# New rules for a build-time planner that orders the in-projection and the delta rule

## The chip, the cores and the metric

The kernel runs on one core of a Trainium2 chip. The metric is device time in microseconds for one execution, taken as the median of several runs. The profile is one such execution, recorded by the hardware profiler.

The engines are named as in the profile: PE is TensorE (matmul), DVE is VectorE, ACT is ScalarE, POOL is GpSimd, SP is SyncE, which here only issues DMAs. Each engine works through its own list of instructions in order; between engines there are semaphores.

## The reference

One residual block on a sequence of 1024 tokens of width 1024, batch 1, all in float32:

```python
mod = c_act @ w_ada + b_ada                       # shift1, scale1, gate1, shift2, scale2, gate2
h = rms_norm(x, norm1_w) * (1 + scale1) + shift1
p = h @ w_in                                      # q, k, v, z (4 heads x 128), a, beta, sc_b, sc_c, sc_h
qkv = silu(causal_depthwise_conv(p[:, q|k|v], width 4))
g = -exp(A_log) * softplus(a + dt_bias);  beta = sigmoid(b)
o = gated_delta_rule_chunked(l2(q), l2(k), v, g, beta)    # chunks of 64
o = rms_norm(o, gdn_norm_w) * silu(z)
y_sc = sc_b * causal_depthwise_conv(sc_c * sc_h, width 3)
x = x + gate1 * (concat[o, y_sc] @ w_out)
h = rms_norm(x, norm2_w) * (1 + scale2) + shift2
x = x + gate2 * ((silu(h @ w_gate) * (h @ w_up)) @ w_down)     # inner width 2816
return rms_norm(x, norm_f_w)
```

Inside the delta rule each chunk needs the inverse of a unit lower triangular 64 x 64 matrix (`triangular_solve` in the reference):

```python
lmat = where(strict, (k * beta) @ k.T * decay, 0)
tmat = triangular_solve(lmat, eye, lower=True, unit_diagonal=True)
u = tmat @ (v * beta);  w = tmat @ (k * beta * exp(g))
# scan over chunks:
v_new = u - w @ S;  out = q_dec @ S + attn @ v_new;  S = S * exp(g_last) + k_dec.T @ v_new
```

## The kernel before

The sequence is worked in two halves of 512 tokens, called hf 0 and 1. Activations stand transposed, 128 channels on the partitions and 512 tokens along a row. A float32 product is made of three fp32r matmuls of 512 columns, on a high and a low part of each operand: `h` holds the normalised input's parts, `u` (or `L`, `wu`) a weight's. A weight block is loaded as `raw`, cast to its high part on ACT or DVE, and the low part is a DVE subtraction.

The program has three parts. A short start and the feed-forward part (lines L87 and L88) are issued in an order that is written by hand. Between them, for roughly the first 475 us, the in-projection, the delta rule, the out-projection and the conditioning vectors are written as some forty small tasks (`ab_phase`, `stage_a`, `gdn`, `merge`, `output`, `load_y`, `coordinator` and so on). Each is ordinary code that asks the class `Sim` before every instruction. `Sim` keeps a clock for each engine while the kernel is built, prices every instruction (`cost`), works out when its operands are ready (`ready`) and when it could start (`start_of`), and issues next the instruction that can start first, by the tasks' priorities among near ties (`run`). `MARGIN` is a time that it adds to what a PE instruction waits for. So the numbers in `Sim` do nothing on the chip; they only set the order in which each engine gets its instructions. All instructions of this part have one line in the profile, that of the common helper: L452 before, L464 after.

The steps which the prediction follows:

- `ab_phase(hf)` multiplies `h` with the few columns for a and b (tile `ab`), copies the result out of PSUM as `raw`, turns it (`abt`), and computes the decay `G` from it on DVE, ACT and PE.
- `stage_a` makes each head's chunk matrices `kk`, `qk`, its decays from `WQ` (loaded from `g_scr`), `L` and `at`, with exponentials on ACT.
- `gdn(hf)` waits for all heads, loads the 16 x 16 x 64 diagonal blocks into `A` and inverts them by forward substitution on DVE (pairs of rows `qs<-A` and `A<-A,qs`, 30 steps). The result is turned, for hf 0 by DMAs through DRAM (`dx` into `xbd`), for hf 1 in `turned` by two DVE transposes and by copies on ACT and POOL. From `xbd` come `DD` (tile `qs`, transposed once more) and `XA` (tile `A`). `merge` then joins the blocks on PE in two levels (`P`, `Q`, `PP`, `Tt`); the first instruction of it on PE is `P<-qs,L`.
- The scan over chunks has on PE `A`, `O`, `V` and `K`. `output` squares `O` on ACT (`jk`, `so`), takes the root on POOL (`ro`), scales `u`, and turns it (`y`).
- `w_out_units` and `load_y` fetch the weights and the rows of y for the out-projection `o<-h,L`; `y_scr` is a scratch in DRAM, the four jobs of `y1` fetch the second half of its first four blocks into `WQ`. `coordinator` opens memory pools and loads `x2`, the input again, for the residual sum.

Of the kernel before, what the change touches and what calls it, by code (L numbers as in the profile page):

```python
# [35 lines left out]
PIPE0 = 8.25  # L36
AHEAD_T = 0.5
HOLD = dict(pe=0.0, dve=0.12, act=0.12, sp=0.0, pool=0.0)
MARGIN = dict(pe=0.6)
BIAS = dict(dve=0.3)  # L40
PR = dict(sums0=0.35, x0=0.1, ada0=0.2, h0=0.3, late=0.31, w0=0.4, acc=0.5, load0=0.0, setup=0.2, hurry=0.5, chain=0, m=1, evac=1.2, a=2, v=2.5, ab=1.2, out=4, h1=1.3, split=3, y0=5, wu=5.5, x2=6, ada=7, fill=9)
TASKS = "z00 q30 q20 s00 z12 z32 z22 z01 q31 q11 q01 q21 s32 s22 s10 s11 s01".split()
# [9 lines left out]
def kernel(  # L52
# [253 lines left out]
    class Sim:  # L306
        ENG = {"pe": "pe", "dve": "dve", "act": "act", "pool": "pool", "sp": "sp"}

        def __init__(self, chain_, start):
            self.chain, self.t, self.table = chain_, dict(start), "Silu"  # L310
            self.acc, self.owner, self.hist = {}, {}, {}
            self.tasks, self.pipe, self.now, self.cur = [], 0.0, 0.0, None
            self.back = threading.Semaphore(0)
            self.lock = []
            self.log, self.idle = [], {}

        def res(self, tag, n, ids=None):
            return Res(self, tag, range(n) if ids is None else ids)

        def own(self, t, res, i, t0=0.0):  # L320
            self.owner[t.tensor.name] = (res, i)
            if t0:
                self.acc[t.tensor.name] = [[0, P, 0, 1 << 30, t0, True, None]]
# [32 lines left out]
        def region(self, ap):  # L356
# [15 lines left out]
                    hi += s * (n - 1)  # L372
            return name, p0, p0 + dims[0][1], lo, hi + 1, ap.space == bass.MemoryType.DRAM

        def cost(self, eng, op, a, k):
            outs, ins = [], []
            pos = [v for v in a if hasattr(v, "tensor")]
            if "out" in k:
                outs.append(k["out"])
            else:  # L380
                outs.append(pos.pop(0))
            ins += pos
            for n, v in k.items():
                if n != "out" and hasattr(v, "tensor"):
                    (outs if n == "accum_out" else ins).append(v)
            o = outs[0]
            n = o.free_size()
            table = None
            if eng == "pe":
                if op == "transpose":  # L390
                    busy = 0.107
                else:
                    fast = ins[1].dtype == F32R
                    busy = max(n * 0.000443, 0.107) if fast else max(n * 0.00168, 0.224)
                lat = busy + 0.30
            elif op == "dma_start":
                busy, lat = 0.44, None
            elif eng == "act":
                big = max([n] + [v.free_size() for v in ins])
                busy = 0.15 + (0.1 if hasattr(k.get("scale"), "tensor") else 0.0) + big * 0.0007 + (0.19 if "accum_out" in k else 0.0)  # L400
                lat = busy + 0.25
                func = [v for v in a if isinstance(v, type(AF.Silu)) and v in (AF.Silu, AF.Exp, AF.Ln)] if op == "activation" else []
                if func:
                    table = str(func[0]).split(".")[-1]
            elif eng == "pool":
                busy = 1.1 if op == "tensor_tensor" else 0.1 + n * 0.0009 if op == "memset" else 0.65 if n >= 256 else 0.5
                lat = busy + 0.15
            else:
                big = max([n] + [v.free_size() for v in ins])
                sb = all(v.space != PSUM for v in outs + ins)  # L410
                if op == "memset":
                    busy = 0.08 + n * 0.0005
                elif sb and op in ("tensor_copy", "tensor_scalar"):
                    busy = 0.08 + n * 0.00062
                else:
                    busy = 0.08 + big * 0.00104 + (0.05 if op == "scalar_tensor_tensor" else 0.0)
                if "accum_out" in k:
                    busy += 0.1
                lat = busy + 0.15
            return outs, ins, busy, lat, table  # L420

        def ready(self, eng, outs, ins):
            t = 0.0
            for w, aps in ((True, outs), (False, ins)):
                for ap in aps:
                    name, p0, p1, f0, f1, dram = self.region(ap)
                    for a in self.acc.get(name, ()):
                        if (w or a[5]) and a[0] < p1 and p0 < a[1] and a[2] < f1 and f0 < a[3]:
                            if eng == "pe" and a[6] == "pe" or dram and w or eng == "dma" and w and a[5] and a[6] == "dma":
                                continue  # L430
                            t = max(t, a[4])
            return t
# [24 lines left out]
        def start_of(self, way):  # L457
            eng, (outs, ins, busy, lat, table), at = way
            if at is None:
                at = way[2] = self.ready("dma" if lat is None else eng, outs, ins) + MARGIN.get(eng, 0.0)  # L460
            t = max(at, self.t[eng])
            return t + 1.28 if table and table != self.table else t

# [33 lines left out]
        def run(self):  # L497
            while True:
# [25 lines left out]
                if lat is None:  # L524
                    run_ = min(n_ for n_ in (ap.ap[-1][1] * 4 for ap in outs + ins))
                    self.pipe = max(t + DMA_T[0], self.pipe) + outs[0].nbytes() / (150e3 if run_ <= 128 else 290e3 if run_ <= 1024 else 380e3)
                    end = rd = self.pipe + DMA_T[1]
                else:
                    end, rd = t + lat, t + busy + 0.1
                self.idle.setdefault(eng, []).append((self.t[eng], t, busy, task["name"], "", outs[0].tensor.name))  # L530
# [310 lines left out]
        spread_cols(RS, rs1, rs_scr)  # L841
        done.add("x1")

    h1_left = list(range(KB))

    def h1_work():
        sim.wait(lambda: "x1" in done)
        while h1_left:
            k = h1_left.pop(0)
            h = h_slot(k, 1)  # L850
            hf = hfs.tile(sp, [P, HT], F32, "hf")
            DVE.scalar_tensor_tensor(hf, x1t[k // 2][:, k % 2], s1c[:, k:k + 1], RS, ALU.mult, ALU.mult)
            ACT.activation(h[:, 0, :], hf, AF.Identity, bias=b1c[:, k:k + 1])
            DVE.scalar_tensor_tensor(h[:, 1, :], hf, b1c[:, k:k + 1], h[:, 0, :].bitcast(F32), ALU.add, ALU.subtract)
            free(hf)
            H[k][1] = h
            if all(H[j][1] is not None for j in range(KB)):
                done.add("h1")
# [135 lines left out]
    M_ORD = (4, 5, 6, 7, 0, 1, 2, 3)  # L994
    sq_acc = []

    held, n_wout = [], [0]

    def ev_o(ps, m):
        sim.wait(lambda: ("x2", m) in done and "g1" in done)  # L1000
        x_ = x2[m][:, 0:HT]
        DVE.scalar_tensor_tensor(x_, ps, g1c[:, m:m + 1], x_, ALU.mult, ALU.add)
# [200 lines left out]
    def gdn(hf):  # L1203
# [32 lines left out]
        for p in range(2):  # L1236
            for c in range(2):
                q = 64 * c + 32
                ecopy(DD[64 * c + 32 * p:64 * c + 32 * p + 32, 0], xbd[0][q:q + 32, p::2, q:q + 32])
        for p in range(2):  # L1240
            for c in range(2):
                q, m, r = 64 * c + 32 - 32 * p, Q_AT[p, c], 64 * c
                POOL.tensor_copy(XA[q:q + 32, :, m:m + 32], xbd[0][r:r + 32, p::2, r:r + 32])
        DVE.transpose(flat(DD[:, 1]), flat(DD[:, 0]))
        for h in heads:
            sim.spawn(merge, PR["m"], hf, h, T, XA, DD)
        sim.wait(lambda: all(("mq", hf, h) in done for h in heads))
# [97 lines left out]
    def w_unit(k, ch, take, out_):  # L1345
# [2 lines left out]
        n_wout[0] += 1  # L1348
        if n_wout[0] == 2 * KB:
            done.add("wout")  # L1350
            for kw, m in held:
                seq("sp", nc.sync.dma_start(**kw))
                done.add(("x2", m))
        hi, lo = take()
        if k < 4:
            escale(hi, r, gnc)
# [25 lines left out]
    def take_lx(n):  # L1382
        def take():
            sim.wait(lambda: all(("uw", 1, h) in done for h in heads))
            if len(xbd) == 1:
                xbd.append(gp.tile([P, 4, HT], F32R, name="wu", tag="xbd", bufs=1))
            return gt("L", (P, HT), F32R), xbd[1][:, n, :]
        return take

    def take_wq():  # L1390
        t = gt("WQ", (P, 2, HT), F32R)
        return t[:, 0, :], t[:, 1, :]

# [16 lines left out]
            sim.spawn(series, PR["wu"], jobs)  # L1410

    def y1():
        sim.wait(lambda: ("chain", 1) in done)
        jobs = [(load_y, k, 1, take_wq) for k in KORD[:4]]
        for _ in range(2):
            sim.spawn(series, PR["y0"], jobs)
# [3 lines left out]
    def coordinator():  # L1420
# [16 lines left out]
            gp.tile([P, 4, P], F32, name=nm("L_0"), tag=f"L{i}", bufs=1)  # L1437
        for i in range(2):
            POOL.memset(xbd[0][:, 8 * i:8 * i + 8, :], 0.0)
        done.add("gp")  # L1440
        sim.wait(lambda: "filled" in done and live[0] == 0 and all(("vt", 1, h) in done for h in heads) and
                 all(("sc", i, hf) in done and ("z", i, hf) in done for i in range(4) for hf in range(2)))
        b1.__exit__(None, None, None)
        pools["x2"] = tc.tile_pool(name="x2p", bufs=1, side="right", reuse_waits="tile")
        x2p = pools["x2"].__enter__()
        for t in range(NT):
            x2.append(x2p.tile([P, D], F32, name=f"x2_{t}", tag=f"x2_{t}"))
        for i, m in enumerate(M_ORD):
            sim.wait(lambda: len(us1) + len(us0) > min(5 + i, 12))
            if i < 2 or "wout" in done:  # L1450
                dma(x2[m], x_t[m])
                done.add(("x2", m))
            else:
                sim.op("sp", "dma_start", lambda **kw: held.append((kw, m)) or [], (), dict(out=x2[m], in_=x_t[m]))

    gp = x2p = b1p = None
    x2 = []
# [1184 lines left out]
```

## Time and profile before

| | us |
|---|---|
| median of 3 runs (lowest, highest) | 1144.19 (1143.35, 1146.99) |
| profiled execution, whole | 1145.62 |
| its span, first to last instruction | 1143.8 |
| PE busy in it | 1126.6 |
| DVE, ACT, POOL busy | 948.6, 612.1, 99.3 |
| mean granted TensorE clock | 0.998 |

A row of the timeline has its start, its length, the engine, the line, the operation, the tile that it writes, the tiles that it reads, and in brackets the idle time of that engine just before it with what ended it. A row may stand for several like instructions (x4). Tile names are those of the program without their numbers. Ends of matmuls are modelled, so two matmuls that follow each other overlap a little in the records.

### The profile page before, as it was taken

To read this page: it belongs to the slowest core of one execution; us is meant where nothing else is said; L and a number is where in the kernel's file an instruction comes from. 1 tells how busy PE (TensorE), PEld (TensorE's weight loads), DVE (VectorE), ACT (ScalarE), POOL (GpSimd) and SP (SyncE) were. 2 spreads that over 40 slices of the span, in tenths; PEclk is the share of its full clock that TensorE was granted. 3 is DMA by queue.
4 is the path that set the end of the run, shared out by engine and by line. 5 is a ranking of instruction groups with operands and counts; after the bars stand their busy time and mean duration, and the time that the engine had idled before them with its cause. 6 is when DMAs were issued, how large, how long until landed. Compare 5 with 4: busy or idle time off the path is not lost.

```text
span 1143.8 us, 17102 instructions
## 1 busy us (share of the span) xinstructions
PE 1126.6 (98%) x5660; PEld 951.2 (83%) x5660; DVE 948.6 (83%) x1909; ACT 612.1 (54%) x1372; POOL 99.3 (9%) x150
## 2 busy tenths in 40 slices
PE   9998999999999999999999999999999999999997
PEld 7887888898888897888888888888888888888885
DVE  7798879889989856699988998878888886689976
ACT  7686863649733643255544544545454476454344
POOL 0010100101100201000010010101010000000302
PEclk9999999999999999999999999999999999999999
DMA  9933256655355472440367667876677599669933
GB/s 367 353 102 102 79 171 192 177 180 183 116 180 174 159 279 68 74 148 19 139 181 210 171 187 177 233 197 162 183 207 200 138 329 362 206 177 355 289 136 147
DMA packets 164978, 214.65 MB, mean 188 GB/s; under 512 B 52589, under 2 KB 81305, under 8 KB 164889
## 3 DMA queue, kind: packets, MB, share of 16 engines
q1 hardware_dynamic: 155832, 198.69, 53.4%
q0 software_dynamic: 7712, 14.42, 8.0%
q8 instruction: 44, 0.72, 0.3%
q10 hardware_dynamic: 1344, 0.46, 0.2%
q14 instruction: 46, 0.37, 0.1%
HBM read 163.94 MB, written 60.58 MB: 196 GB/s over the span
## 4 chain that ended last, share of the span: by engine, by line
PE 90%; ACT 3%; DVE 3%; DMA 1%; issue 1%; POOL 0%; SPq 0%; ACTq 0%; DVEq 0%
PE acc L87 36%; PE acc L452 24%; PE dn L87 16%; PE o L87 4%; PE o L452 3%; DVE xo L88 1%; PE O L452 1%; PE P L452 1%; PE Q L452 1%; PE V L452 1%; PE qk L452 1%; DMA raw<-y_scr 1%; PE K L452 1%; PE A L452 1%; ACT L L452 1%
## 5 line engine op out<-in xcount | busy, mean ns | idle before, releaser
L452 PE MATMUL acc<-h,u 128*128 128x512 f32 x1200 | 293.6, 396 | 0.0
L452 PEld LDWEIGHTS acc<-h,u 128*128 128x128 f32 x1200 | 220.4, 188 | 42.4
L87 PE MATMUL acc<-h,hl 128*128 128x512 f32 (+1 forms) x540 | 109.1, 353 | 0.1
L87 PEld LDWEIGHTS acc<-h,hl 128*128 128x128 f32 x540 | 90.3, 189 | 15.1 <-issue 0.5
L87 PE MATMUL acc<-h,u 128*128 128x512 f32 (+1 forms) x516 | 100.4, 345 | 0.0
L87 PE MATMUL acc<-T,hl 128*128 128x512 f32 x408 | 97.6, 391 | 0.3 <-DVE T L88 0.3
L87 PEld LDWEIGHTS acc<-h,u 128*128 128x128 f32 x516 | 84.7, 189 | 12.6
L87 PE MATMUL acc<-T,u 128*128 128x512 f32 x384 | 91.2, 390 | 0.0
L87 PE MATMUL dn<-h,h 128*128 128x512 f32 x396 | 90.7, 389 | 0.0
L87 PEld LDWEIGHTS acc<-T,hl 128*128 128x128 f32 x408 | 75.2, 188 | 15.8 <-DVE T L88 0.8
L87 PEld LDWEIGHTS dn<-h,h 128*128 128x128 f32 x396 | 74.4, 188 | 15.4
L87 PEld LDWEIGHTS acc<-T,u 128*128 128x128 f32 x384 | 71.0, 188 | 14.1
L452 ACT CAST u<-raw 128x512 fp32r<-128x512 f32 x68 | 41.9, 619 | 53.9 <-PE acc L452 46.5
L452 DVE TENSOR_TENSOR u<-raw,u 128x512 fp32r<-128x512 f32 x82 | 56.6, 692 | 6.4 <-ACT u L452 5.8
L88 ACT COPY L<-acc 128x256 f32<-128x256 f32 x68 | 25.3, 372 | 64.4 <-PE acc L87 64.0
L88 ACT CAST h<-rw 128x512 fp32r<-128x512 f32 x60 | 35.1, 619 | 40.8 <-PE dn L87 26.3
L88 DVE TENSOR_TENSOR xo<-xo,dn 128x512 f32<-128x512 f32 x66 | 44.9, 684 | 14.1 <-PE dn L87 13.6
L452 DVE SCALAR_TENSOR_TENSOR cv<-pr,cols_a,cv 128x512 f32<-128x512 f32 x72 | 53.0, 749 | 1.5 <-ACT cv L452 1.3
L88 DVE TENSOR_TENSOR h<-rw,h 128x512 fp32r<-128x512 f32 x60 | 39.7, 687 | 15.6 <-ACT h L88 15.6
L452 DVE SCALAR_TENSOR_TENSOR raw<-raw,cb 128x512 f32<-128x512 f32 x64 | 43.8, 686 | 4.3 <-DMA raw<-in_w_mod_dram 3.9
L88 DVE TENSOR_TENSOR cc<-cc,acc 128x512 f32<-128x512 f32 x66 | 41.3, 646 | 4.9 <-PE acc L87 4.9
L88 ACT COPY cc<-acc 128x512 f32<-128x512 f32 x64 | 35.2, 585 | 19.0 <-PE acc L87 19.0
(399 smaller groups left out, 2193.0 us busy)
## 6 DMA issues: line engine op xcount, KB each, us to landing
raw<-in_w_in_dram SPq DMA_DIRECT2D x82, 256.0 KB, 3.4
am_scr<-cc SPq DMA_DIRECT2D x75, 256.0 KB, 2.2
raw<-in_w_mod_dram SPq DMA_DIRECT2D x64, 256.0 KB, 3.1
rw<-am_scr SPq DMA_DIRECT2D x53, 256.0 KB, 5.3
R<-in_w_gate_dram SPq DMA_DIRECT2D x22, 512.0 KB, 5.1
R<-in_w_up_dram SPq DMA_DIRECT2D x22, 512.0 KB, 5.9
rw<-bm SPq DMA_DIRECT2D x43, 256.0 KB, 5.3
wa<-in_w_mod_dram SPq DMA_DIRECT2D x16, 512.0 KB, 9.3
```

Source lines behind the costliest of these rows:

```text
L87: return call(*a, **k)
L88: ins = call(*a, **k)
L452: ins = call(*a, **k)
```

## The change

Nothing that is computed changes. The edits are of three kinds.

1. The planner's rules. `ready` has each engine wait for all accesses of another engine to the same PSUM tile, whichever part of the tile they touch, and lets ACT, DVE and POOL overwrite what they wrote themselves without waiting. `start_of` keeps a DMA back until the eighth last has landed. `gone` tells when memory comes free that a new pool takes over, for the first pool's slots, for `x2` and for the second use of `xbd`. `MARGIN` for PE goes from 0.6 to 1.0.
2. The planner's prices: dearer POOL roots and strided copies, strided copies on ACT, strided DVE transposes, activations with a bias, and `tensor_scalar`; cheaper short sums on ACT.
3. The tasks: `y1` starts when all weights of the out-projection are under way, and waits for the end of the second chain only before it takes `WQ`; `x2` loads are issued by the coordinator as out-projection tiles begin, instead of being held in a list; in `gdn` the transpose of `DD` is written ahead of the copies to `XA`.

```diff
-MARGIN = dict(pe=0.6)
+MARGIN = dict(pe=1.0)
...
+        def gone(self, aps):
+            return max([a[4] for ap in aps for a in self.acc.get(ap.tensor.name, ())] + [self.now])
...
+            apart = lambda ap, n: n >= 256 and ap.space != PSUM and abs(ap.ap[-1][0]) > 1 and ap.ap[-1][1] > 1
...
-                busy = 0.15 + (0.1 if hasattr(k.get("scale"), "tensor") else 0.0) + big * 0.0007 + (0.19 if "accum_out" in k else 0.0)
+                busy = 0.15 + 0.09 * sum(hasattr(k.get(n_), "tensor") for n_ in ("scale", "bias")) + big * 0.0007
+                busy += (0.06 if n <= P else 0.19) if "accum_out" in k else 0.3 if apart(ins[0], n) else 0.0
...
-                busy = 1.1 if op == "tensor_tensor" else 0.1 + n * 0.0009 if op == "memset" else 0.65 if n >= 256 else 0.5
+                busy = 1.35 if op == "tensor_tensor" else 0.1 + n * 0.0009 if op == "memset" else 1.03 if apart(ins[0], n) else 0.7 if n >= 256 else 0.42
...
-                    busy = 0.08 + big * 0.00104 + (0.05 if op == "scalar_tensor_tensor" else 0.0)
+                    busy = 0.08 + big * 0.00104 + (0.05 if op in ("scalar_tensor_tensor", "tensor_scalar") else 0.0)
+                if op == "transpose" and apart(ins[0], n):
+                    busy += n * 0.00104
...
                     for a in self.acc.get(name, ()):
+                        if ap.space == PSUM and a[6] not in (eng, None):
+                            t = max(t, a[4])
+                            continue
                         if (w or a[5]) and a[0] < p1 and p0 < a[1] and a[2] < f1 and f0 < a[3]:
-                            if eng == "pe" and a[6] == "pe" or dram and w or eng == "dma" and w and a[5] and a[6] == "dma":
+                            if eng == "pe" and a[6] == "pe" or dram and w or eng == "dma" and w and a[5] and a[6] == "dma" or \
+                                    w and a[6] == eng and eng in ("act", "dve", "pool"):
                                 continue
...
-                at = way[2] = self.ready("dma" if lat is None else eng, outs, ins) + MARGIN.get(eng, 0.0)
+                at = way[2] = max(self.ready("dma" if lat is None else eng, outs, ins) + MARGIN.get(eng, 0.0), 0.0 if lat else self.landed[-8])
...
+        DVE.transpose(flat(DD[:, 1]), flat(DD[:, 0]))
         for p in range(2):
             for c in range(2):
                 q, m, r = 64 * c + 32 - 32 * p, Q_AT[p, c], 64 * c
                 POOL.tensor_copy(XA[q:q + 32, :, m:m + 32], xbd[0][r:r + 32, p::2, r:r + 32])
-        DVE.transpose(flat(DD[:, 1]), flat(DD[:, 0]))
...
     def take_wq():
+        sim.wait(lambda: ("chain", 1) in done)
         t = gt("WQ", (P, 2, HT), F32R)
...
     def y1():
-        sim.wait(lambda: ("chain", 1) in done)
+        sim.wait(lambda: "wout" in done)
...
-            if i < 2 or "wout" in done:
-                dma(x2[m], x_t[m])
-                done.add(("x2", m))
-            else:
-                sim.op("sp", "dma_start", lambda **kw: held.append((kw, m)) or [], (), dict(out=x2[m], in_=x_t[m]))
+            if i > 1:
+                sim.wait(lambda: "wout" in done or len(begun) >= i)
+            dma(x2[m], x_t[m])
+            done.add(("x2", m))
```

What this does to the order is read from the two programs' instruction lists. On ACT, at the second `ab_phase` (`raw<-ab` copies its result out of PSUM; `WQ`, `L`, `at` are decays of the first half's heads), the list before is

```order
L452 COPY ch_1190<-acc_1130 128x512
L452 ACTIVATE h_1_275_1178<-hf_1179,b1c 128x512
L452 ACTIVATE h_1_271_1156<-hf_1157,b1c 128x512
L452 CAST u_1217<-raw_1194 128x512
L452 ACT_TABLE_LOAD
L452 ACTIVATE WQ_1254<-WQ_1254 128x512
L452 ACTIVATE L_1246<-L_1246,G_1090 128x128
L452 COPY raw_1284<-ab_1236 128x512
```

and after

```order
L464 COPY ch_1189<-acc_1130 128x512
L464 CAST u_1214<-raw_1192 128x512
L464 ACTIVATE h_1_275_1179<-hf_1180,b1c 128x512
L464 COPY raw_1284<-ab_1242 128x512
L464 CAST u_1293<-raw_1218 128x512
L464 ACTIVATE cv_1315<-ch_1189,cols_a 128x512
L464 ACT_TABLE_LOAD
L464 ACTIVATE WQ_1260<-WQ_1260 128x512
```

The copy out of PSUM has moved from behind the table load and two exponentials to a place ahead of them.

On PE, at the start of `merge` for the second half, before:

```order
L452 MATMUL acc_4216<-h_1_210_842,u_4123 128x512 x3
L452 MATMUL acc_4216<-h_1_211_843,u_4123 128x512 x3
L452 MATMUL acc_4216<-h_1_227_930,u_4123 128x512 x3
L452 MATMUL acc_4216<-h_1_235_979,u_4123 128x512 x3
L452 MATMUL acc_4216<-h_1_246_1038,u_4151 128x512 x3
L452 MATMUL acc_4216<-h_1_263_1118,u_4151 128x512 x3
L452 MATMUL acc_4216<-h_1_271_1156,u_4151 128x512 x3
L452 MATMUL P_4261<-qs_4212,L_2860 128x128 x2
```

and after:

```order
L464 MATMUL acc_4219<-h_1_213_858,u_4126 128x512 x3
L464 MATMUL acc_4219<-h_1_214_859,u_4126 128x512 x3
L464 MATMUL P_4232<-qs_4179,L_2877 128x128 x2
L464 MATMUL P_4233<-qs_4179,L_2878 128x128 x2
L464 MATMUL P_4234<-qs_4179,L_2879 128x128 x2
L464 MATMUL P_4235<-qs_4179,L_2880 128x128 x2
L464 MATMUL acc_4219<-h_1_232_955,u_4126 128x512 x2
```

`P` comes after 6 matmuls of the last accumulation instead of 21.

On DVE, after the second half's last chunk (`x_5` is the residual sum's second tile, `WQ<-raw` the cast of a loaded row block of y, `so` the scaled square sums, `ro` their roots), before:

```order
L452 SCALAR_TENSOR_TENSOR x_5_4601<-o_4678,mod_c,x_5_4601 128x512
L452 CAST WQ_4748<-raw_4743 128x512
L452 TENSOR_TENSOR WQ_4748<-raw_4743,WQ_4748 128x512
L452 TENSOR_TENSOR sq_4685<-sq_4685,raw_4766 128x512
L452 SCALAR_TENSOR_TENSOR so_4739<-so_4739,nq_3623 128x4
L452 SCALAR_TENSOR_TENSOR so_4740<-so_4740,nq_3313 128x4
L452 TENSOR_TENSOR WQ_4779<-raw_4777,WQ_4779 128x512
L452 TENSOR_TENSOR WQ_4750<-raw_4744,WQ_4750 128x512
L452 TENSOR_TENSOR u_3497<-u_3497,ro_4745 128x512
```

and after:

```order
L464 SCALAR_TENSOR_TENSOR x_5_4589<-o_4674,mod_c,x_5_4589 128x512
L464 CAST WQ_4760<-raw_4601 128x512
L464 CAST WQ_4761<-raw_4615 128x512
L464 TENSOR_TENSOR sq_4679<-sq_4679,raw_4749 128x512
L464 TENSOR_TENSOR WQ_4760<-raw_4601,WQ_4760 128x512
L464 TENSOR_TENSOR WQ_4761<-raw_4615,WQ_4761 128x512
L464 SCALAR_TENSOR_TENSOR so_4758<-so_4758,nq_3595 128x4
L464 SCALAR_TENSOR_TENSOR so_4759<-so_4759,nq_3309 128x4
L464 TENSOR_TENSOR u_3504<-u_3504,ro_4764 128x512
```

The two `raw` blocks that are cast here are now loaded ahead of all eight `x2` loads on SP (before, behind them), and the other two blocks' subtractions have moved behind the first scaling of `u`.

More of the change, by code (lines that the diff above doesn't have):

```diff
@@ L314, in __init__ @@
             self.lock = []
-            self.log, self.idle = [], {}
+            self.log, self.idle, self.made, self.landed = [], {}, {}, [0.0] * 8
         def res(self, tag, n, ids=None):
@@ L320, in own @@
         def own(self, t, res, i, t0=0.0):
+            self.made.setdefault(res.tag, []).append(t)
             self.owner[t.tensor.name] = (res, i)
@@ L527, in run @@
                     end = rd = self.pipe + DMA_T[1]
+                    self.landed.append(end)
                 else:
@@ L842, in h1_load @@
         done.add("x1")
-    h1_left = list(range(KB))
+    h1_left, h1_t = list(range(KB)), [RS]
     def h1_work():
@@ L855, in h1_work @@
             free(hf)
+            h1_t.append(hf)
             H[k][1] = h
@@ L995 @@
     sq_acc = []
-    held, n_wout = [], [0]
+    n_wout, begun = [0], []
     def ev_o(ps, m):
+        begun.append(m)
         sim.wait(lambda: ("x2", m) in done and "g1" in done)
@@ L1350, in w_unit @@
             done.add("wout")
-            for kw, m in held:
-                seq("sp", nc.sync.dma_start(**kw))
-                done.add(("x2", m))
         hi, lo = take()
@@ L1386, in take @@
                 xbd.append(gp.tile([P, 4, HT], F32R, name="wu", tag="xbd", bufs=1))
+                sim.acc[xbd[1].tensor.name] = [[0, P, 0, 1 << 30, sim.gone(xbd[:1]), True, None]]
             return gt("L", (P, HT), F32R), xbd[1][:, n, :]
@@ L1439, in coordinator @@
             POOL.memset(xbd[0][:, 8 * i:8 * i + 8, :], 0.0)
+        left = sim.gone(x1t + h1_t)
+        for res in GP.values():
+            res.slots = [(max(t0, left), i) for t0, i in res.slots]
         done.add("gp")
@@ L1445, in coordinator @@
         x2p = pools["x2"].__enter__()
+        left = sim.gone([t for tag in ("pr", "cv", "vT", "qkT") for t in sim.made[tag]])
         for t in range(NT):
             x2.append(x2p.tile([P, D], F32, name=f"x2_{t}", tag=f"x2_{t}"))
+            sim.acc[x2[-1].tensor.name] = [[0, P, 0, 1 << 30, left, True, None]]
         for i, m in enumerate(M_ORD):
             sim.wait(lambda: len(us1) + len(us0) > min(5 + i, 12))
-            if i < 2 or "wout" in done:
-                dma(x2[m], x_t[m])
-                done.add(("x2", m))
-            else:
-                sim.op("sp", "dma_start", lambda **kw: held.append((kw, m)) or [], (), dict(out=x2[m], in_=x_t[m]))
+            if i > 1:
+                sim.wait(lambda: "wout" in done or len(begun) >= i)
+            dma(x2[m], x_t[m])
+            done.add(("x2", m))
     gp = x2p = b1p = None
```

## The prediction

> **What bounds the kernel now.** I read the page's first lines, then the waits of PE, then a table of windows, then the timeline at each wait.
>
> ```profile
> span 1143.8 us, 17102 instructions
> PE 1126.6 (98%) x5660; PEld 951.2 (83%) x5660; DVE 948.6 (83%) x1909; ACT 612.1 (54%) x1372; POOL 99.3 (9%) x150
> PE 90%; ACT 3%; DVE 3%; DMA 1%; issue 1%; POOL 0%; SPq 0%; ACTq 0%; DVEq 0%
> ```
>
> PE is busy 98% of the span and holds 90% of the chain that ended last. A new order of the same instructions can only win what PE waits. The list of PE's waits (total us, times, longest) has these rows that belong to the planned part; its other rows (the start, and L87) the change does not touch:
>
> ```profile
> PE abt L452 <- ACT raw L452: 3.6, 2, 3.4
> PE P L452 <- DVE qs L452: 1.7, 1, 1.7
> PE y L452 <- DVE u L452: 1.2, 2, 1.0
> PE G L452 <- ACT jk L452: 0.7, 1, 0.7
> ```
>
> That is 7.2 us in six waits. The windows (length, then busy time and count of PE, PEld, DVE, ACT, POOL, granted clock, DMA) put them in three stretches; the long feed-forward stretch, last row, has none:
>
> ```profile
> 100.00:150.00 50.00, 45.66 (x244) 37.92 (x244) 39.80 (x123) 37.68 (x125) 6.84 (x10) 1.00 0.30 89
> 350.00:400.00 50.00, 48.31 (x262) 41.15 (x261) 45.04 (x104) 27.69 (x72) 8.60 (x10) 1.00 0.55 174
> 400.00:450.00 50.00, 48.76 (x283) 42.03 (x282) 31.66 (x68) 22.01 (x60) 4.92 (x4) 1.00 0.58 201
> 600.00:1000.00 400.00, 400.00 (x2085) 344.48 (x2084) 331.14 (x565) 207.41 (x407) 26.54 (x32) 1.00 0.75 212
> ```
>
> A wait costs a little more than its idle time. In the timeline at the first half's P, six full matmuls start 1.36 us before P, 0.227 us each, but the six are drawn 1.52 us long: the last one's drawn end overlaps what could run next by 0.16 us. I add 0.16 us to each wait: 7.2 + 6 x 0.16 = 8.2 us is all there is to win.
>
> **The change part by part.** No arithmetic is added or removed; the planner runs when the kernel is built. PE has as many instructions as before, ACT gains one table load (1.28 us in the next fence, on an engine that is 54% busy), and some casts change between ACT and DVE. What counts is the order.
>
> *The abt waits.* The timeline of the long one (start, length; idle time before and its releaser in brackets):
>
> ```profile
> 106.06 2.03 SPq L452 DMA_DIRECT2D WQ<-g_scr  x4
> 109.40 0.69 DVE L452 TENSOR_TENSOR L<-WQ,ct 128x512 f32<-128x512 f32 x1 [3.50 <-DMA WQ<-g_scr]
> 110.85 1.28 ACT L452 ACT_TABLE_LOAD   x1 [5.27 <-DVE at L452]
> 112.68 0.39 ACT L452 ACTIVATE L<-L,G 128x128 f32<-128x128 f32 x1
> 112.97 0.56 ACT L452 COPY raw<-ab 128x512 f32<-128x512 f32 x1
> 113.59 0.66 PE L452 MATMUL abt<-ident,raw 128*128 128x128 f32 x4 [3.41 <-ACT raw L452]
> ```
>
> ACT works in order. It sits idle 5.27 us for a DVE row that itself waited 3.50 us for a load, then loads its table, takes two exponentials, and only then copies ab out of PSUM, which PE has needed since about 110.2. In the new order (first pair of order rows) that copy stands ahead of the table load and of both exponentials. What stands right ahead of it now are casts, activations and a copy that do not hang on that load; ACT's 5.27 us of idle time hold them. PE meets abt two matmuls later (0.45 us). The 3.41 + 0.16 = 3.6 us go. Bounds: all of it back (if one of the casts ahead waits for a weight load as long as L did), or all gone; nearest is the idle row, so gone. The short abt wait, at 58, goes too (0.2 + 0.16 = 0.4): two of the casts ahead of its copy on ACT now come after it, and PE meets abt two matmuls later.
>
> *G.* PE stopped because ACT had not released a bank:
>
> ```profile
> 136.68 0.40 PE L452 MATMUL G<-g,ct 128*128 128x16 f32 x2 [0.72 <-ACT jk L452]
> ```
>
> In the new order G stands some 15 us later, behind a bank whose readers end well before. That gives 0.7 + 0.16 = 0.9. With the two abt waits that makes 4.9 us by time 150.
>
> *P of the second half* (the start of merging the chunk inverses) is moved 15 matmuls up PE's order (second pair of order rows). The timeline:
>
> ```profile
> 369.10 0.69 DVE L452 TENSOR_TENSOR ch<-acc,ch 128x512 f32<-128x512 f32 x1
> 370.41 1.14 DVE L452 STREAM_TRANSPOSE qs<-A 64x512 f32<-64x512 f32 x1
> 372.10 0.68 DVE L452 TENSOR_TENSOR h<-raw,h 128x512 fp32r<-128x512 f32 x1
> 372.70 1.14 DVE L452 STREAM_TRANSPOSE turn<-A 64x512 f32<-64x512 f32 x1
> 374.42 2.07 POOL L452 COPY xbd<-turn 32x256 f32<-32x256 f32 x2
> 374.84 1.14 DVE L452 TENSOR_TENSOR u<-raw,u 128x512 fp32r<-128x512 f32 x1
> 380.46 0.43 DVE L452 STREAM_TRANSPOSE qs<-qs 128x256 f32<-128x256 f32 x1
> 380.95 1.27 PE L452 MATMUL P<-qs,L 128*128 128x128 f32 x9 [1.69 <-DVE qs L452]
> ```
>
> Set the clock at the end of the accumulation that DVE's ch row waits for (369.06). PE then has 30 matmuls before P instead of 45, so it wants P at +6.8 (it wanted it at +10.2 and got it at +11.9). In the new DVE order both big transposes stand before that ch row; between ch and the transpose qs<-qs there are seven rows of 512 columns, 0.61 to 0.68 us from start to start where POOL leaves them alone, 1.07 where rows beside POOL's copies ran 1.13 to 1.15 long. Seven such rows and the transpose give +5.1 to +7.9. ACT's and POOL's copies out of turn, started at its end, are over by about +5.5 by the lengths shown. So P comes between on time and 1.1 us late; I take 0.3 late, since only some rows beside POOL ran long (h at 372.10 did not). Of 1.7 + 0.16 = 1.9 us, 1.6 are won.
>
> [...]
>
> *P of the first half* is moved up 23 matmuls, 5.2 us, and this is where a wait can appear that was not there:
>
> ```profile
> 162.18 0.09 DVE L452 MEMSET A<- 64x32 f32 x1
> 197.97 0.18 DVE L452 TENSOR_TENSOR A<-A,qs 64x30 f32<-64x30 f32 x1
> 207.79 1.52 PE L452 MATMUL acc<-h,u 128*128 128x512 f32 x6
> 208.17 0.43 DVE L452 STREAM_TRANSPOSE qs<-qs 128x256 f32<-128x256 f32 x1
> 209.15 0.49 PE L452 MATMUL P<-qs,L 128*128 128x128 f32 x3
> ```
>
> Before, 36.0 us of forward substitution on DVE and 10.4 us of transposing through memory ended 0.55 us ahead of P. Now PE wants P at 209.15 - 5.2 - 4.9 = 199.05. The chain starts earlier by the abt wait and by some order ahead of it (I count 4.5 us, start 157.6); between memset and last A row DVE has 82 rows instead of 88, the six missing all of 512 columns (6 x 0.64 = 3.8, so 32.2 us); the tail is one or two fillers shorter (9.7). That ends at 199.5: a new wait of 0.5 us. Bounds: none, and 5.0 if the substitution still takes 36.0 and the tail 10.4. I take 0.5, from the row count.
>
> *The loads of the second half's y rows.* The transpose y waits for u, u for POOL's root, that for so on DVE, and so stands behind a cast of a late load:
>
> ```profile
> 424.90 1.83 SPq L452 DMA_DIRECT2D raw<-y_scr  x4
> 426.48 0.59 ACT L452 COPY u<-O 128x512 f32<-128x512 f32 x1 [2.10 <-PE O L452]
> 428.55 0.75 DVE L452 SCALAR_TENSOR_TENSOR x<-o,mod_c,x 128x512 f32<-128x512 f32 x1 [6.15 <-PE o L452]
> 431.36 0.43 DVE L452 CAST WQ<-raw 128x512 fp32r<-128x512 f32 x1 [2.06 <-DMA raw<-y_scr]
> 433.04 0.23 DVE L452 SCALAR_TENSOR_TENSOR so<-so,nq 128x4 f32<-128x4 f32 x2
> 433.35 2.54 POOL L452 TENSOR_TENSOR ro<-so,nhalf 128x4 f32<-128x4 f32 x2 [38.22 <-DVE so L452]
> 435.68 0.66 PE L452 MATMUL y<-ident,u 128*128 128x128 f32 x4 [1.05 <-DVE u L452]
> ```
>
> Two of the four loads now go on SP ahead of the eight loads of x and land before O ends. From the end of O the chain is then: copy 0.5, four square sums 1.2, so 0.2, first root 1.5, product 0.7, with 0.3 of queueing 4.4 us; PE has 27 matmuls between O and y, 6.1 us. The x loads start two transfers later; DVE waited 6.15 us for PE and not for x. The two loads left behind can hold the second y by about 0.1. Of 1.2 + 2 x 0.16 = 1.5 us, 1.4 are won; bounds 0 (the cast still late) and 1.5.
>
> *The rest of the planned order.* Every other step moves too. The old plan left 8.2 us of waits that its own numbers had not foreseen, in some 430 us; the new one has more margin on PE and other prices. I count 1.0 us of new waits, between none and 3 (a wait like abt's).
>
> Sum: -3.6 - 0.4 - 0.9 - 1.6 - 1.4 + 0.5 + 1.0 = -6.4. The profiled run took 1145.62, its span of 1143.8 and 1.8 around it, 1.43 over the median of 1144.19; it becomes 1139.2, and on the median's scale 1137.8.
>
> One thing would make the 3.41 us idle dearer than it looks, a colder clock behind it. The window after it shows none:
>
> ```profile
> 113.60:117.00 3.40, 3.40 (x19) 2.92 (x20) 2.86 (x11) 3.40 (x11) 0.00 (x0) 1.00 0.43 142
> ```
>
> The granted clock is 1.00 there. [...]
>
> **The rivals.** (a) The first half's P takes the wait over: substitution does not shorten, the wait is 5.0 instead of 0.5, and the time is 1142.3. For it: P had only 0.55 us to spare. Against: the six missing rows. (b) Waits only move: the new order loses elsewhere as much as the old, 7 us of new waits instead of 1.0, time 1143.8. For it: each of the old waits sat where the plan had foreseen none. Against: the rules added are those whose lack one can name at abt and G, a bank held by another engine's reader. (c) Slower: PE's order runs ahead of the delta rule. If both chains end as late as before (208.60 for the first; 11.8 after its accumulation for the second), the P waits are 209.15 - 0.55 - 199.05 = 9.6 and 11.8 - 6.8 = 5.0, against 0.5 and 0.3 in my sum: 13.8 more, 1151.6. It decides when the two together exceed my 0.8 by 9.8 us. Against: the chain must then have lost the 4.9 us by which PE itself is earlier.
>
> **How the numbers follow.** Within 0.3% (3.4 us) a change cannot be told from none: 1140.8 to 1147.6. Likeliest, as summed, 66%: 1137.8, by itself 1135 (all 8.2 us won is 1136.0, and the lowest run shown lies 0.8 under its median) to 1140.8 (three us of new waits and one at P). (a) 14%, (b) 11%, (c) 9%. Leaving out (c) and the worse part of (b), the range is 1134.8 to 1144.5. Faster: the likeliest and a few per cent of (a), 0.69; same: the rest of (a) and (b), 0.22; slower 0.09.
>
> **What would show it.** Right: no PE wait on ACT raw at abt; PE busy of the window 100 to 150 near 49 us; y without a wait on u; the cast of WQ ahead of x's second update without idle time on a DMA. Wrong: a row P <- DVE qs or <- ACT qs of several us near 200; a P row near 372; a new row for kT, qT, kk or qk behind ACT or DVE, where banks now change hands in turn.

## The result, and the profile after

Six runs of the changed kernel have a median of 1135.84 us (1134.72 to 1137.40); six of the kernel before, on the same chip, 1144.85. The ratio is 0.9921, with a 95% interval of 0.9907 to 0.9934: faster by 9.0 us, between 7.6 and 10.6 (0.8%). The forecast was a time lower by 6.4 us.

The profiled execution after took 1134.72 us. Its page:

```profile
span 1132.9 us, 17110 instructions
PE 1122.9 (99%) x5660; PEld 950.8 (84%) x5660; DVE 943.3 (83%) x1900; ACT 618.7 (55%) x1382; POOL 99.4 (9%) x150
PE 93%; DVE 2%; ACT 1%; issue 1%; POOL 1%; DMA 1%; SPq 0%; ACTq 0%; DVEq 0%
```

PE has the same 5660 matmuls and now holds 93% of the chain that ended last instead of 90%. What is left of PE's waits is short enough to be shown whole (total us, times, longest):

```profile
PE heat L87 <- POOL eps_c L88: 1.5, 1, 1.5
PE acc L464 <- ACT h L464: 0.6, 1, 0.6
PE Q L464 <- POOL A L464: 0.3, 1, 0.3
PE acc L87 <- DVE T L88: 0.3, 1, 0.3
PE ps L87 <- DVE raw L88: 0.2, 1, 0.2
```

Of the planned part's four rows (abt, P, y, G: 7.2 us) none is left; one row has come, Q, with 0.3 us. The second row belongs to the start, the others to parts that the change does not touch. The windows that showed the old waits (columns as before: length, then PE, PEld, DVE, ACT, POOL, granted clock, DMA):

```profile
100.00:150.00 50.00, 50.00 (x276) 42.74 (x275) 38.47 (x119) 42.77 (x143) 7.36 (x12) 1.00 0.33 101
350.00:400.00 50.00, 49.68 (x286) 43.23 (x285) 44.37 (x104) 30.76 (x75) 10.50 (x9) 1.00 0.61 192
400.00:450.00 50.00, 50.00 (x272) 42.95 (x271) 27.74 (x59) 18.93 (x54) 5.37 (x5) 1.00 0.51 174
```

PE was idle for 4.34, 1.69 and 1.24 us of these windows, 7.27 in all; now 0, 0.32 and 0. So 7.0 us of idle time went, but between the two profiles 10.9 us of span. Of these, 9.2 us lie between PE's first matmul on `h` and its first one in the hand-ordered part behind the plan (15.71 to 464.53 us before, 14.07 to 453.66 after), where the order was planned anew. The other 1.6 us lie ahead of that first matmul. There `ps` and the row `heat` behind it, in the same hand-written order, took 3.78 and 3.57 us before and 2.85 and 2.84 after, and PE waited 0.69 and 0.17 us for `ps`; against that stands the wait of 0.6 us for the first `h`, which the profile before doesn't have. Such differences come between executions of one order (that wait for `h` is 1.8 us in a kernel below whose order on PE is the same), so the profiles overstate the gain and the medians are the better size.

### The profile page after: what moved, and what is told of

Read it like the earlier page. It is cut to its first block, busy times and chain, and to the rows that moved or that the text cites. A ratio compares the mean times of both kernels' runs of the same rounds, so it can differ in the third digit from the quotient of the medians.

```text
span 1132.9 us, 17110 instructions
## 1 busy us (share of the span) xinstructions
PE 1122.9 (99%) x5660; PEld 950.8 (84%) x5660; DVE 943.3 (83%) x1900; ACT 618.7 (55%) x1382; POOL 99.4 (9%) x150
## 4 chain that ended last, share of the span: by engine, by line
PE 93%; DVE 2%; ACT 1%; issue 1%; POOL 1%; DMA 1%; SPq 0%; ACTq 0%; DVEq 0%
PE acc L87 36%; PE acc L464 25%; PE dn L87 17%; PE o L87 4%; PE o L464 4%; PE O L464 1%; DVE xo L88 1%; PE Q L464 1%; PE ab L464 1%; PE V L464 1%; PE kk L464 1%; PE qk L464 1%; PE K L464 1%; PE A L464 1%; PE P L464 0%
## 5 line engine op out<-in xcount | busy, mean ns | idle before, releaser
L464 ACT CAST u<-raw 128x512 fp32r<-128x512 f32 x63 | 38.9, 620 | 49.7 <-PE acc L464 44.4
```

What stands on the lines that cost most here:

```text
L464: ins = call(*a, **k)
```

## The experiments

The edits fall into kinds: the margin (M); the prices in `cost` (C); the turns in PSUM and an engine's own overwrite in `ready` (T); and the tasks (K), that is `y1`'s early loads, `x2` loaded by the coordinator and the order of `DD` and `XA`. Each was tried alone on the kernel before, and each was undone alone in the changed one. The count of transfers under way and the shared memory told to the builder are a fifth kind, which was not tried by itself: it is in all four kernels with one kind undone and in none of those with one kind alone. Part of what the whole set gains may be its doing, and no run here shows how much.

**One kind alone.** The margin:

```diff
-MARGIN = dict(pe=0.6)
+MARGIN = dict(pe=1.0)
```

> The kernel before with the margin of 1.0 us on PE as its only change. In its order the copy raw<-ab of the second half stands ahead of the table load and the exponentials (row 136 against 138), G comes 25 PE instructions later, P and y stand as before and the y rows are loaded behind x2. Theory of named waits: the abt wait (3.6) and the G wait (0.9) go, the waits of P (1.9) and y (1.5) stay, so about 1140.3. Rival, scatter: every new plan of this planner loses about as much as the old one, wherever it loses it, so within 2 us of before, and waits of 7 us or more in the list.

The prices alone (the pieces of `cost` in the diff above, nothing else):

> The kernel before with the new prices only. The copy raw<-ab still stands behind the table load and one exponential, G comes later, P of the second half 11 PE instructions earlier, y loads behind x2. Named waits: abt stays at about 3 us, G goes, P and y stay within 1 us of what they were, so about 1143.5. Scatter: within 2 us of before, with waits in places that the old plan had not.

The turns alone; without `x2` loaded by the coordinator this order can't be finished, so that is in it too:

```diff
+                        if ap.space == PSUM and a[6] not in (eng, None):
+                            t = max(t, a[4])
+                            continue
...
+                                    w and a[6] == eng and eng in ("act", "dve", "pool"):
```

> The kernel before with the rule of turns in a PSUM tile (and no waiting for one's own writes), and with x2 loaded by the coordinator, without which this plan does not come to an end. The copy raw<-ab stands behind the table load, G comes 75 PE instructions later, P of the first half 29 earlier and of the second 8 earlier. Named waits: abt stays (3.6), G goes (0.9), y stays (1.5), the first P may wait up to 1 us, so 1143.5 to 1145. If the turns were what mended abt, as rival (b) of the prediction had it, abt is gone and the time is under 1141.

The tasks alone:

```diff
-        sim.wait(lambda: ("chain", 1) in done)
+        sim.wait(lambda: "wout" in done)
...
+            if i > 1:
+                sim.wait(lambda: "wout" in done or len(begun) >= i)
...
+        DVE.transpose(flat(DD[:, 1]), flat(DD[:, 0]))
         for p in range(2):
...
-        DVE.transpose(flat(DD[:, 1]), flat(DD[:, 0]))
```

> The kernel before with the new tasks only: y rows loaded before x2, x2 loaded by the coordinator, the transpose of DD ahead of the POOL copies. The copy raw<-ab and G stand as before, P of the second half 13 PE instructions earlier. Named waits: abt (3.6) and G (0.9) stay, y (1.5) goes, P keeps 1 to 2 us, so about 1143. Scatter: within 2 us of before, the y wait somewhere else.

And a change that means nothing, to see what any other order is worth under the old rules:

```diff
-BIAS = dict(dve=0.3)
+BIAS = dict(dve=0.29)
```

> The kernel before with one number moved that means nothing (the planner's bias against DVE, 0.29 instead of 0.30), to see how far a new plan under the same rules scatters. The copy raw<-ab stands behind the table load as before. Scatter: within 3 us of before either way, with a list of waits in other places; the waits named in the prediction, but abt, gone or moved.

| alone | median us | before, same chip | ratio (95%) | longest wait in the planned part |
|---|---|---|---|---|
| M | 1141.21 | 1144.22 | 0.9970 (0.9958 to 0.9982) | 0.8 |
| C | 1148.44 | 1144.22 | 1.0033 (1.0018 to 1.0048) | 3.2 |
| T | 1147.96 | 1144.22 | 1.0031 (1.0018 to 1.0044) | 3.6 |
| K | 1147.59 | 1144.22 | 1.0023 (1.0013 to 1.0032) | 2.7 |
| bias 0.29 | 1146.22 | 1144.46 | 1.0014 (1.0005 to 1.0023) | 3.7 |

Only the margin gains by itself, a third of the whole. I had expected about 1140.3 of it. The three other kinds came out worse than I had expected: the prices (1143.5), where I had not seen y's wait, the turns (1143.5 to 1145), where I had not seen the wait of the scan's `K`, and the tasks (1143). The rows of the waits of PE show where these kernels wait. Prices alone:

```profile
PE y L460 <- DVE u L460: 3.9, 2, 3.2
PE abt L460 <- ACT raw L460: 3.0, 1, 3.0
```

Turns alone:

```profile
PE abt L460 <- ACT raw L460: 3.8, 2, 3.6
PE K L460 <- ACT A L460: 3.1, 1, 3.1
PE P L460 <- DVE qs L460: 1.7, 1, 1.7
```

The bias, where the wait on abt is gone and another stands at 296 us, nearly as long:

```profile
PE acc L456 <- ACT pr L456: 3.7, 1, 3.7
```

The sum of such rows does not explain the losses by itself. In the planned part the rows add up to 7.2 us before, 8.3 for the prices, 9.8 for the turns, some 7 for the tasks and 6.1 for the bias. In the profiles part of the rest goes with a lower clock behind long waits (last section). But over all its runs the clock of the kernel with the tasks alone is no lower than that of the kernel before (0.9973 and 0.9971), so why it is 3.4 us slower stays open.

So a long wait is not tied to abt. The kernel before and the four other plans that keep the old margin and have at most one kind of edit each contain one or two waits of 2.7 us or more; which instruction has it depends on the plan. And naming the rule that was broken did not mend it: with the turns told, G's wait goes, but abt still stands behind the table load on ACT, with 3.6 us. The margin, which knows nothing of banks or tables, moved it:

```profile
PE P L456 <- DVE xbd L456: 0.8, 2, 0.6
PE P L456 <- DVE qs L456: 0.8, 1, 0.8
PE vT L456 <- DVE L L456: 0.7, 1, 0.7
PE qk L456 <- DVE kt L456: 0.6, 1, 0.6
```

These are the longest rows of the planned part with the margin alone: several small waits in place of abt's and P's.

**One kind undone in the changed kernel.** The edits are those above, backwards.

> The changed kernel with the margin of PE back at 0.6 us, all else as changed. The copy raw<-ab still stands ahead of the table load, P of the second half comes 18 PE instructions later and P of the first half 7 earlier, y as in the changed kernel. If the margin is only one of several ways to the same order at abt and G, the time is within 2 us of the changed kernel. If the margin carries the gain, as the run with the margin alone suggests, waits of 0.3 to 1 us appear in many places and the time is 1139 to 1141.

> The changed kernel with the old prices. abt stands as in the changed kernel; P of the second half comes 49 PE instructions later and y 32 later. With the old prices the plan thinks that strided copies on POOL and ACT are short. Named waits: the tail of the second half is late, a P or y wait of 1 to 2 us, 1138 to 1140. Together only: 1140 or more, with a wait over 2.5 us and a clock of 0.997 or less.

> The changed kernel with the old tasks (y rows loaded behind x2, x2 held in a list, DD turned after the POOL copies). In its order P of the second half stands 20 PE instructions earlier than in the changed kernel, where it had 0.64 us to spare, and y 17 earlier. Named waits: P waits up to 3.9 us, y 1.5, so 1139 to 1142, and the clock falls in a part of the runs. If the tasks did nothing, within 1.5 us of the changed kernel.

> The changed kernel without the rule of turns in a PSUM tile. abt and G stand as in the changed kernel, P of the second half 18 PE instructions later, y 8 later. If the four kinds of edit are only worth something together, waits of 1 us or more come back, 1139 or more. If turns decide little by now, within 1.5 us of the changed kernel (1134.5 to 1137.5), with waits of a few tenths where a bank changes hands.

| undone | median us | over after | ratio to before (95%) | longest wait in the planned part |
|---|---|---|---|---|
| M | 1136.94 | 1.1 | 0.9932 (0.9917 to 0.9946) | 0.7 |
| C | 1137.16 | 1.3 | 0.9938 (0.9924 to 0.9953) | 0.7 |
| K | 1137.80 | 2.0 | 0.9941 (0.9926 to 0.9956) | 0.9 |
| T | 1139.59 | 3.8 | 0.9952 (0.9935 to 0.9968) | 2.2 |

For M, C and K the interval overlaps that of the changed kernel, 0.9907 to 0.9934: M and C may be worth a microsecond or two, or nothing. The four runs with the tasks undone (1137.64 to 1138.19) all lie above the six of the changed kernel (up to 1137.40), so the tasks are probably worth something. The margin, which gains alone, is hardly missed here. Only the turns stand clear of the interval. Without them two instructions of PE that need what ACT copies wait, in a profile of the slowest of the four runs (1142.07):

```profile
PE K L460 <- ACT A L460: 2.2, 1, 2.2
...
PE Q L460 <- ACT qs L460: 1.3, 1, 1.3
```

The kinds do not add up. Alone they give -3.0, +4.2, +3.7 and +3.4 us, in sum +8.3; all together, with the fifth kind, gave -9.0. With one of C, T and K the plan still has a wait of about 3 us somewhere; with any three of the four kinds that hold the turns, none above 0.9 once PE has its first `h`. Where I had expected waits of 1 to 4 us, for C and K undone, the longest were 0.7 and 0.9. No kernel tried is below the changed one.

**What a wait costs.** Taking abt's wait away was the largest term of the sum. To measure one, I put it back into the changed kernel at the same place, in three lengths: a small tile is copied and then cleared n times on POOL, and PE must transpose it ahead of the second half's abt. It adds one matmul and n + 1 POOL instructions; the order of all others on PE, ACT and POOL is the same in the traces.

```diff
         pt = bank(chb, "abt")
+        if hf == 1:
+            late = cst.tile([P, 64], F32, name="late", tag="late")
+            sim.chain("pool", nc.gpsimd.tensor_copy(late, abT[:, 0:64]))
+            for _ in range(10):
+                sim.chain("pool", nc.gpsimd.memset(late, 0.0))
+            sim.chain("pe", nc.tensor.transpose(pt[0:64, 0:P], late, ident))
```

> The changed kernel with one PE wait put back by hand near the second abt: a small tile is copied and then cleared 10 times on POOL, and PE turns it (the result is overwritten) before it may go on. No other order changes. By the lengths of small POOL rows PE should idle some 2.5 us. If a wait costs what PE idles, the median is 1138.3 and the mean granted clock stays at 0.998 to 0.999. If a wait also lets the clock fall, a part of the runs shows 0.997 or less and the time is up to 1.7 us more in them.

> The same with 18 clears, some 3.7 us of idle PE, which is what the kernel before had at abt. Idle time alone: 1139.5, clock as in the changed kernel. With a falling clock: about as many runs at 0.995 to 0.997 as the kernel before has (23 of 29 at 0.998 or less), median near 1141.

> The same with 32 clears, some 5.8 us of idle PE. Idle time alone: 1141.6. With a falling clock: every run at 0.997 or less, and 1.7 us or more on top, near 1143.5.

| n | idle put in, us | median us | over after | ratio to before (95%) | mean clock of the runs |
|---|---|---|---|---|---|
| 0 (after) | 0 | 1135.84 | 0 | 0.9921 (0.9907 to 0.9934) | 0.9987 |
| 10 | 2.7 | 1140.46 | 4.6 | 0.9965 (0.9952 to 0.9977) | 0.9975 |
| 18 | 4.3 | 1143.51 | 7.7 | 0.9991 (0.9981 to 1.0001) | 0.9960 |
| 32 | 7.3 | 1146.41 | 10.6 | 1.0011 (1.0002 to 1.0021) | 0.9948 |

The series were taken on different chips, and the median of the kernel before differs between them by up to 0.6 us, so "over after" is open by that much beside the intervals. The idle times are longer than planned (2.5, 3.7 and 5.8), and so are the times. The expectation for 18 clears counts the clocks wrongly: 25 of those 29 runs of the kernel before have a clock of 0.998 or less, and 17 one of 0.995 to 0.997. The idle times are those of the put-in row in each list of waits of PE:

```profile
PE abt L783 <- POOL late L782: 2.7, 1, 2.7
```

```profile
PE abt L783 <- POOL late L782: 4.3, 1, 4.3
...
PE Q L464 <- POOL A L464: 1.3, 1, 1.3
```

```profile
PE abt L783 <- POOL late L782: 7.3, 1, 7.3
```

Each costs 1.9 to 3.4 us more than its idle time (4.6 - 2.7, 7.7 - 4.3, 10.6 - 7.3). In its profile the middle kernel waits elsewhere too: 1.3 us at Q instead of 0.3, and 0.7, 0.4 and 0.2 us in three short rows between 46 and 60 us. The rest goes with the granted clock: 0.0012, 0.0027 and 0.0039 below that of the changed kernel, times some 1140 us, are 1.4, 3.1 and 4.4 us. These are upper bounds, since a lower clock costs nothing while PE is idle; with n = 32 the clock is at half from 114.31 us on, and PE waits until 117.25.

For the shortest, the profile shows no fall of the clock behind the put-in wait, but one at 15.59 to 19.01 us, after a wait for the first `h` of 1.8 us, in an order on PE that is the same as in the kernel after. This execution (1140.49) took 5.8 us more than the profiled one of the kernel after: 2.7 of the put-in wait, 1.1 by which PE's first matmul on `h` starts later (15.16 us, not 14.07), and 1.7 for half of 3.4 us at the lower clock, 5.5 in all. So there the put-in wait itself cost little more than its idle time, and the extra came from the start. How much of the extra of the other five runs came from there stays open.

## Why the prediction was right, and where it was mis-sized

The direction, the mechanism (only PE's waits can be won) and the side on which it came out were as forecast. Point by point:

*abt and G, 4.9 us.* Right. ACT now copies first and loads its table after (timeline: start, length, instruction; in brackets idle time before and releaser):

```profile
106.99 0.59 ACT L464 COPY raw<-ab 128x512 f32<-128x512 f32 x1 [4.02 <-PE ab L464]
109.01 0.60 PE L464 MATMUL abt<-ident,raw 128*128 128x128 f32 x4
109.59 1.28 ACT L464 ACT_TABLE_LOAD   x1
```

The copy waits for PE, not PE for the copy: PE comes to abt 1.4 us after its end. There is no wait at G.

*The second half's P, 1.6 of 1.9 us won.* P was not 0.3 late; its transpose ended at 367.51, 0.6 us ahead of it:

```profile
362.30 5.01 POOL L464 COPY xbd<-turn 32x256 f32<-32x256 f32 x2
365.64 1.15 DVE L464 SCALAR_TENSOR_TENSOR cv<-ch,cols_a,cv 128x512 f32<-128x512 f32 x1
367.06 0.45 DVE L464 STREAM_TRANSPOSE qs<-qs 128x256 f32<-128x256 f32 x1 [0.27 <-issue]
368.14 1.95 PE L464 MATMUL P<-qs,L 128*128 128x128 f32 x16
368.39 2.43 POOL L464 COPY A<-xbd 32x256 f32<-32x256 f32 x4
370.87 0.60 PE L464 MATMUL Q<-qs,A 128*128 128x128 f32 x3 [0.32 <-POOL A L464]
```

I had priced what DVE and POOL cost each other on DVE's rows alone. Rows of both ran long: a DVE row beside POOL is again 1.15 us long, and POOL's pair of copies takes 5.01 us instead of 2.07 (shortest, median and longest of the two copies in ns):

```profile
L464 POOL COPY xbd<-turn x2: 1037/2486/3936, 362.3 to 366.3; 32x256 f32<-32x256 f32 x2
```

The first takes 3.94 us, while DVE works without a gap, the second 1.04; before, each took 1.01 to 1.02. Here it was POOL's copy that ran long most. For the kernel before I had named the row h at 372.10, 0.68 us, as one that did not run long beside POOL's copies; but the POOL copy that it ran beside (the first of two `xbd<-qs`, 371.61 to 373.30) took 1.69 us, the second 1.02. No run varies this alone, so what decides which of the two runs longer is not shown. What came late next were POOL's copies for `XA`, and PE waits 0.32 us for them at Q.

*The first half's P, +0.5.* The step that failed, in the harmless direction: no wait.

```profile
152.76 0.09 DVE L464 MEMSET A<- 64x32 f32 x1
186.51 0.18 DVE L464 TENSOR_TENSOR A<-A,qs 64x30 f32<-64x30 f32 x1
194.69 0.45 DVE L464 STREAM_TRANSPOSE qs<-qs 128x256 f32<-128x256 f32 x1 [0.32 <-ACT qs L464]
196.58 0.60 PE L464 MATMUL P<-qs,L 128*128 128x128 f32 x4
```

The chain starts at 152.8, not 157.6; 1.6 us of that is the earlier first matmul on `h` in this execution. The substitution took 33.9 us where the row count gave me 32.2, and the transposing through memory 8.4 instead of 9.7, so the two errors nearly cancel, and the earlier start leaves 1.4 us to spare. Rival (a), this P late by 5 us, and (c), PE ahead of both chains, had that start wrong.

*The second half's y, 1.4.* Right:

```profile
419.12 0.76 DVE L464 CAST WQ<-raw 128x512 fp32r<-128x512 f32 x2
419.83 0.57 ACT L464 COPY u<-O 128x512 f32<-128x512 f32 x1
422.03 0.16 DVE L464 SCALAR_TENSOR_TENSOR so<-so,nq 128x4 f32<-128x4 f32 x1 [0.18 <-ACT jk L464]
422.35 1.03 POOL L464 TENSOR_TENSOR ro<-so,nhalf 128x4 f32<-128x4 f32 x1 [3.05 <-DVE so L464]
423.71 0.68 DVE L464 TENSOR_TENSOR u<-u,ro 128x512 f32<-128x512 f32 x1
425.74 0.60 PE L464 MATMUL y<-ident,u 128*128 128x128 f32 x4
```

The casts of the late loads run without idle time on a DMA, before the scale. From the end of O at 419.8 the product is there after 4.6 us (forecast 4.4), and PE after 5.9 (6.1).

*The unseen rest, +1.0.* Mis-sized: 0.3 us of idle time, 0.5 with the restart that I counted. With the P waits (0 for the first, all 1.9 won for the second) the sum of the prediction's own terms becomes -8.2 + 0.5 = -7.7 instead of -6.4, at the edge of the measured 7.6 to 10.6.

*What is left, some 1.3 us,* points to a term that the prediction had at nothing: it took the list of waits, which shows idle time from 0.15 us up, for all there is to win. In the two profiles, neither of which shows a lower clock in the planned part, 7.0 us less idle time went with 9.2 us less time. I compared the time from one PE instruction's start to the next with the lower quartile for the same two shapes in all traces. In the planned part, steps late by over 0.3 us (7 before, 1 after) make 8.2 us of the difference, which is some 0.2 us beyond the idle time for each of six waits, close to my 0.16. Steps late by 0.04 to 0.3 us (121 before, 106 after) make 1.5 us more. And other executions of the kernel before pay with the clock, which the prediction dismissed on the evidence of one window: over 63 runs its mean granted clock is 0.9970, where the changed kernel's is 0.9987. That is 1.9 us at most (0.0017 x 1143). The six of the 63 with a clock of 0.999 took 1143.36 on average, the mean of all is 1144.43: 1.1 us, the cleaner figure. How the 1.3 us divide between the two is not settled; they are no more than the interval's half-width.

*Rival (b), that waits only move,* was half true. It describes the prices, the turns and the tasks alone, and the meaningless edit, but not the margin, whose waits add up to 3.5 us. Against it I had held that the lack of the rules could be named at abt and G; the run with the turns alone shows that this argument was wrong for abt. The forecast came out without that argument, because its terms were read from the new order itself; why the whole set clears the waits is not shown.

## What to carry to other kernels

In an order made by a model of the machine, a wait can mark the place where the model's errors happened to meet, and mending the rule that one can name there may move the wait elsewhere, as it did here: judge a set of rules by the longest wait of the whole plan, and try a general margin on the bounding engine too; here it was the only kind that gained alone, though the full set hardly missed it. When PE is the bound, price a wait by more than its idle time (the three put in here cost 1.9 to 3.4 us more), count the short delays that a list of waits leaves out, and look at the mean clock of many runs, not at one window of one trace, before calling the rest nothing. Where the rows of two engines ran long beside each other, ask what each would lose, not only the one that stands on the path: here POOL's copy took 3.94 us instead of 1.02.

## What the hardware showed

Eleven waits of PE in these traces have a stretch at half clock behind them, of 3.41 or 6.83 us. In the windows below the last three columns are granted clock, DMA share and GB/s. With the tasks alone, after a wait of 2.72 us at abt:

```profile
111.45 1.12 PE L456 MATMUL abt<-ident,raw 128*128 128x128 f32 x4 [2.72 <-ACT raw L456]
```

```profile
112.20:114.20 2.00, 2.00 (x7) 1.62 (x6) 2.00 (x9) 2.00 (x8) 0.00 (x0) 0.50 0.21 77
```

With the turns undone, before and after the end of the 2.2 us at K, at 416.64:

```profile
414.64:418.05 3.41, 1.41 (x10) 1.38 (x11) 0.97 (x2) 1.71 (x3) 0.00 (x0) 1.00 1.05 413
418.05:421.46 3.41, 3.41 (x15) 3.15 (x15) 0.91 (x4) 0.59 (x1) 0.00 (x0) 0.50 0.92 365
```

With 4.3 us put in at abt, and, with the turns alone, after 3.1 us at K, where nothing happens:

```profile
111.73:115.14 3.41, 1.26 (x4) 1.07 (x5) 0.00 (x0) 0.00 (x0) 1.52 (x11) 0.50 0.00 0
115.14:118.55 3.41, 3.41 (x12) 2.72 (x11) 1.29 (x2) 2.74 (x4) 0.00 (x0) 0.50 0.01 2
```

```profile
421.80:426.00 4.20, 4.20 (x31) 3.90 (x32) 1.95 (x6) 1.22 (x2) 0.00 (x0) 1.00 0.97 394
```

Eight of the eleven falls behind a wait last 3.41 us, which costs about 1.7 us, half of that, where PE works all through. The other three, after 2.7 (tasks alone), 4.3 and 7.3 us at abt, last 6.83. Falls followed waits of 1.8, 1.9 and 2.0 (at the start), 2.2, 2.7, 3.0, 3.2, 3.6, 3.7, 4.3 and 7.3 us; none followed 2.7 (put in), 3.1 and, in the kernel before, 3.4.

So its length does not settle what a wait does to the clock. In these traces what followed goes with the wait's place: each trace records when the granted clock changed, and the times between these changes are whole multiples of 3.413 us. Full clock lasts 1129.81 us in the profile before, 331 of them, and 1122.99 in the one after, 329; with the prices alone 324.27 us lie between the two falls, 95. I cut the time at full clock into pieces of 3.413 us, counted from such a change. Ahead of the kernel's end, all nine pieces in which PE was idle for 2.0 us or more were followed by half clock, and none with 1.75 us or less was. Between these, 1.79 and 1.87 us at the start were followed by it, and 1.87 us in the kernel before was not. The wait of 3.41 us in the kernel before lies across two such pieces, with 1.54 us in one and 1.87 in the other (PE busy 1.88 and 1.54), and the clock stayed at 1.00 in both:

```profile
108.30:111.72 3.42, 1.88 (x9) 1.23 (x7) 2.32 (x4) 0.87 (x1) 0.00 (x0) 1.00 0.98 280
111.72:115.13 3.41, 1.54 (x9) 1.37 (x10) 3.41 (x7) 3.40 (x10) 0.00 (x0) 1.00 0.13 47
```

The pieces lie differently in each trace: the record of full clock starts at 9.32 us in the profile before and at 5.46 in the one after, and `ps` and the `heat` behind it are longer before (3.78 and 3.57 us, against 2.85 and 2.84). Whether this is also why other executions of the kernel before show a lower clock (0.9970 on average over 63 runs) is not shown: no run here varied the place of a wait alone.
